# A second DRAM copy of the RWKV values, laid out by head of the pair, from which the recurrence loads

## The chip, the cores and the metric

One NeuronCore of a Trainium2 chip runs the whole layer. The metric is device microseconds (us) of one execution, the median over several runs. TensorE (PE) does the matrix products, VectorE (DVE), ScalarE (ACT) and GpSimd (POOL) the elementwise work, and SyncE (SP) issues most DMAs; ACT issues some of the stores. All DMAs of the core run on the same 16 DMA engines.

## The reference, cut to what matters

One layer of a hybrid decoder: dilated sliding-window attention and RWKV-7 time mixing run in parallel on the same 1024 tokens x 1024 features, are merged by sigmoid gates, and a squared-ReLU MLP follows. The change touches the values `v` of the RWKV part: 16 heads of 64 features, kept as 8 pairs of heads. Per head the recurrence is

```
r, k, v, fw, fa, fg = split(token_shift(f_rwkv))
def step(state, inp):
    sa = einsum('bhij,bhj->bhi', state, -kk_t)
    state = (state * w_t[:, :, None, :]
             + sa[..., None] * (kk_t * a_t)[:, :, None, :]
             + v_t[..., None] * k_t[:, :, None, :])
    y_t = einsum('bhij,bhj->bhi', state, r_t)
...
bonus = sum(r * k * r_k, axis=-1, keepdims=True) * v
y = (layernorm_per_head(y) + bonus) * g
```

so `v` is read twice: in the recurrence, and later for the bonus term of the output.

## The kernel before, in words

The kernel is written in Bass with a tile framework. The order of TensorE and GpSimd is as the program writes it (`manual_schedule`); the order of VectorE, ScalarE and SyncE is chosen by a scheduler at build time. The program's order comes from `weave` (line 62), which takes steps of a main generator and puts steps of side generators between them.

Stages, with their place in the profiled execution: input norm and low-rank columns (to about 90 us); stage 1, the RWKV projections, eight iterations m = 0 to 7, one per pair of heads (about 90 to 404 us); attention with the inverses of the chunk matrices beside it (to 830 us); the recurrence, `Chain`, 16 chunks of 64 tokens, woven into gate and branch products (about 839 to 1104 us); merge, output projection and MLP (to the end).

Stage 1: `Project.project(m)` (line 376) runs three dense products per m (k, r, v) and `finish(m - 1)` (line 416) is the side generator beside it. In `finish` the 128 value features of a pair, token-minor after the projection, are turned by TensorE transposes to token-major in PSUM (`flip`), four 128-token tiles at a time (h = 0, 1). ScalarE copies them to the tile `VT` (line 436, one buffer: a second copy waits until the stores from the first have landed) and issues the store to `V_d` (line 437). `finish` goes on to the score blocks, which DVE masks into `sc` (line 463) and SyncE stores to `AK_d` and `TB_d` (lines 464, 465). Weight tiles `raw` (line 170, three buffers) are loaded by SyncE and split by ScalarE (`whi`, line 41) and VectorE (`wlo`, line 42).

`V_d` is [1024 tokens, 1024 features]; feature = m*128 + head-of-pair*64 + i. In stage 1 a row of a store is 128 floats (512 B).

The recurrence: `Chain.load(c)` (line 840) issues eight DMAs on SyncE for chunk c: per head of the pair hp the blocks `U` from `AR_d` and `AK_d` (64 partitions each, one run of 4 KB per partition) and the values `SV` (64 partitions: 64 tokens, 8 pairs, 64 floats), and then `TB` and `BKT` (128 partitions, 4 KB runs). In `SV` each partition takes eight runs of 64 floats (256 B), since the two heads of a pair alternate in `V_d`. The tiles have two buffers, so the load for chunk c + 2 waits for the products of chunk c. `chunk(c)` (line 858) begins with products of `SV` and `U` (line 874). Every second chunk `norm(J)` (line 901) reads `V_d` by whole rows (`vt`, line 908), and `post(J)` (line 929) turns the result and stores it to `O_d` from ScalarE (line 956); the tile `y2` that this store reads is written by the next `norm` (line 918) and the next `post` (line 953), which wait until the store has landed.

## Time and profile before

| What | us |
|---|---|
| median of 3 runs | 1954.45 |
| lowest and highest of the 3 | 1944.74, 1958.83 |
| the profiled execution's own time | 1958.2 |
| its span in the profile | 1956.5 |

The mean granted TensorE clock of the profiled execution is 0.972 of full speed. The span is the time from the first to the last recorded instruction; what lies around it is 1.7 us. A row of the profile names a line of the kernel, the engine, and output<-input by the program's tile names; a wait row names the engine that waited, its line, what ended the wait, the total in us, the number of times, and the longest.

### The profile page before, as it was taken

What the parts mean: (1) busy time and instruction counts of PE and PEld (TensorE: products, weight loads), DVE (VectorE), ACT (ScalarE), POOL (GpSimd) and SP (SyncE); (2) the same over time, 40 slices, a digit from 0 to 9 for tenths busy, and PEclk for the clock granted to TensorE, in tenths of its full rate; (3) what the DMA queues carried; (4) which work ended last, traced back from release to release, by engine and by line L of the source; (5) the groups of instructions that cost most, each with busy time, mean ns of one, the idle gap of its engine ahead of it and who ended that gap; (6) DMA issues with size and microseconds to landing.
All of it is one profiled execution on the core that took longest, in us unless ns stands there. A gap on an engine that the chain in (4) does not pass through costs nothing.

```text
span 1956.5 us, 30888 instructions
## 1 busy us (share of the span) xinstructions
PE 1850.8 (95%) x12183; PEld 1509.2 (77%) x12183; DVE 1230.8 (63%) x1857; ACT 793.7 (41%) x1379; POOL 307.4 (16%) x398
## 2 busy tenths in 40 slices
PE   8999999999999999978888899989999998999996
PEld 7888888887787887666666788767888887888885
DVE  6777777734324324436566654668777776776877
ACT  7533333323534525312222333336666655433342
POOL 2011111126141507013333300310000000000001
PEclk9999999999998999989998999999999999999998
DMA  6355556652242241399898454436454447453225
GB/s 181 92 138 139 148 151 153 153 136 69 52 141 55 69 103 40 82 240 235 209 221 208 141 197 136 148 112 229 141 162 143 153 153 241 144 187 136 87 98 182
DMA packets 324914, 283.83 MB, mean 145 GB/s; under 512 B 84926, under 2 KB 275488, under 8 KB 324384
## 3 DMA queue, kind: packets, MB, share of 16 engines
q1 hardware_dynamic: 261984, 247.76, 44.5%
q10 hardware_dynamic: 60672, 26.75, 5.1%
q0 software_dynamic: 2112, 7.34, 1.1%
q8 instruction: 96, 1.57, 0.3%
q14 instruction: 50, 0.41, 0.1%
HBM read 184.70 MB, written 96.57 MB: 144 GB/s over the span
## 4 chain that ended last, share of the span: by engine, by line
PE 76%; DMA 9%; DVE 5%; issue 4%; POOL 3%; ACT 2%; SPq 1%; ACTq 0%; DVEq 0%; POOLq 0%
PE fx L1400 16%; PE fx L1252 14%; PE pd L209 12%; PE pd L211 12%; PE pd L213 12%; DMA O_d<-y 3%; DMA SV<-V_d 2%; PE pm L460 2%; DMA U<-AK_d 1%; PE pm L430 1%; PE po L694 1%; POOL X L515 1%; SPq L501 1%; POOL tmp L514 1%; PE ppt L679 1%
## 5 line engine op out<-in xcount | busy, mean ns | idle before, releaser
L1400 PE MATMUL fx<-w2s,x 128*128 128x512 f32 (+1 forms) x1362 | 307.8, 388 | 5.9 <-DVE w2s L42 4.1
L209 PE MATMUL pd<-hhi,whi 128*128 128x512 f32 (+1 forms) x880 | 300.9, 419 | 0.4 <-DVE Q L590 0.4
L1400 PEld LDWEIGHTS fx<-w2s,x 128*128 128x128 f32 x1362 | 254.9, 189 | 59.0 <-DVE w2s L42 4.4
L211 PE MATMUL pd<-hlo,whi 128*128 128x512 f32 (+1 forms) x880 | 276.9, 392 | 1.0 <-DVE mv L125 1.0
L213 PE MATMUL pd<-hhi,wlo 128*128 128x512 f32 (+1 forms) x880 | 276.0, 391 | 0.0
L42 DVE TENSOR_TENSOR wlo<-raw,whi 128x512 fp32r<-128x512 f32 (+2 forms) x164 | 113.5, 726 | 169.9 <-ACT whi L41 167.4
L211 PEld LDWEIGHTS pd<-hlo,whi 128*128 128x128 f32 x880 | 167.6, 190 | 37.0 <-DVE mv L125 1.3
L213 PEld LDWEIGHTS pd<-hhi,wlo 128*128 128x128 f32 x880 | 167.8, 191 | 35.9
L1252 PE MATMUL fx<-xh,wop 128*128 128x512 f32 x600 | 187.7, 390 | 2.6 <-ACT e L1256 1.6
L209 PEld LDWEIGHTS pd<-hhi,whi 128*128 128x128 f32 x880 | 152.4, 191 | 33.3 <-issue 8.6
L41 ACT CAST whi<-raw 128x512 fp32r<-128x512 f32 (+2 forms) x164 | 92.2, 608 | 198.2 <-PE pd L211 147.4
L1252 PEld LDWEIGHTS fx<-xh,wop 128*128 128x128 f32 x600 | 112.6, 188 | 27.1 <-ACT e L1256 2.0
L41 ACT CAST x<-xr 128x1024 fp32r<-128x1024 f32 x56 | 59.0, 1054 | 153.2 <-issue 87.0
L1252 PE MATMUL fx<-xl,wop 128*128 128x512 f32 x300 | 116.8, 389 | 0.0
L42 DVE TENSOR_TENSOR x<-xr,x 128x1024 fp32r<-128x1024 f32 x56 | 68.4, 1222 | 62.4 <-ACT x L41 62.4
L1354 POOL TENSOR_TENSOR rs<-mv,nhalf 128x1 f32<-128x1 f32 x8 | 6.3, 789 | 629.1 <-ACT jk L1365 608.7
L1181 ACT ACTIVATE e<-e 128x512 f32<-128x512 f32 x128 | 80.2, 633 | 31.0 <-DVE e L1276 10.5
L1252 PE MATMUL fx<-mh,wop 128*128 128x512 f32 x240 | 78.1, 395 | 0.2 <-ACT e L1213 0.2
L666 DVE CUSTOM_DVE_ANT_0 sc<-psc,bias 128x128 f32<-128x128 f32 (+1 forms) x96 | 30.1, 348 | 68.5 <-PE psc L661 52.4
L471 ACT COPY BKs<-pm 128x512 f32<-128x512 f32 x32 | 18.8, 588 | 131.0 <-PE pm L469 107.6
L515 POOL TENSOR_TENSOR X<-X,tmp 128x30 f32<-128x30 f32 (+14 forms) x120 | 65.8, 548 | 9.4
L451 POOL TENSOR_TENSOR BKg<-BK,GC 128x512 f32<-128x512 f32 x32 | 38.6, 1206 | 179.8 <-PE pm L469 175.7
(301 smaller groups left out, 3522.3 us busy)
## 6 DMA issues: line engine op xcount, KB each, us to landing
raw<-in_w_in SPq DMA_DIRECT2D x60, 512.0 KB, 4.3
S_d<-e SPq DMA_DIRECT2D x112, 256.0 KB, 2.1
xr<-S_d SPq DMA_DIRECT2D x56, 512.0 KB, 3.4
raw<-in_w_ffn SPq DMA_DIRECT2D x32, 512.0 KB, 5.1
w<-in_w_ffn SPq DMA_DIRECT2D x16, 1024.0 KB, 5.7
xt<-in_x SPq DMA_DIRECT2D x16, 512.0 KB, 5.5
AR_d<-AR SPq DMA_DIRECT2D x8, 1024.0 KB, 7.3
BKT_d<-BKs ACTq DMA_DIRECT2D x32, 256.0 KB, 3.4
```

Of the source, the lines that this page charges most:

```text
L41: nc.scalar.copy(hi, raw)
L42: nc.vector.tensor_sub(lo, raw, hi)
L209: nc.tensor.matmul(o, whi[k], xh[k], start=(k == 0), stop=False)
L211: nc.tensor.matmul(o, whi[k], xl[k], start=False, stop=False)
L213: nc.tensor.matmul(o, wlo[k], xh[k], start=False, stop=(k == kt - 1))
L451: nc.gpsimd.tensor_mul(t, BK[:, csls[b], :], g.GC[:, m, csls[b]].unsqueeze(2).to_broadcast([128, 4, 128]))
L460: nc.tensor.matmul(pair[hp][:, i * 128:(i + 1) * 128], BK[side[hp], cc, :], AR[side[hp], cc, :], start=True, stop=True)
L515: nc.gpsimd.tensor_add(X[:, s + 1:32, 0:s], X[:, s + 1:32, 0:s], tv)
L666: nc.vector.tensor_tensor_reduce(out=sc[:, c0:256], in0=pair[hp][:, c0:256], in1=bias[:, h, c0:256], scale=1.0, scalar=3.0e38, op0=ALU.add ...
L1181: self.g.nc.scalar.activation(t, t, f)
L1252: nc.tensor.matmul(out, op[:, w, k, :], xop[v][:, k, :], start=(n == 0 and not add), stop=(n == 11), skip_group_check=add)
L1400: nc.tensor.matmul(po[:, cols], x[:, xi, ts], w[:, wi, cols], start=(first and m == 0), stop=(last and m == 2), skip_group_check=more)
```

## The change

The values are stored twice. A DRAM tensor `VC_d` [1024 tokens, 2 heads of the pair, 8 pairs, 64] is added. In `finish`, after the store of `VT` to `V_d`, SyncE issues two more stores of the same `VT`, one per head of the pair; each moves 128 partitions x 4 tiles x 64 floats (runs of 256 B, 128 KB in all). Over m = 0 to 7 and h = 0, 1 these are 32 DMAs, 4.2 MB. `Chain.load` takes `SV` from `VC_d`: one run of 512 floats (2 KB) per partition instead of eight runs of 256 B. `norm` goes on reading `V_d`. No computing instruction is added or removed; line numbers after the first insertion shift by 1, after the second by 3, from line 1460 on by 4.

```diff
@@ finish
         vd = g.V_d.rearrange("(j p) c -> p j c", p=128)[:, :, m * 128:(m + 1) * 128]
+        vc = g.VC_d.rearrange("(j p) h m i -> p j h m i", p=128)
...
             nc.scalar.dma_start(vd[:, 4 * h:4 * h + 4, :], VT)
+            for hp in range(2):
+                nc.sync.dma_start(vc[:, 4 * h:4 * h + 4, hp, m, :], VT[:, :, side[hp]])
@@ Chain.load
-        vd = g.V_d[c * 64:(c + 1) * 64, :].rearrange("t (m h i) -> t h m i", m=8, h=2)
+        vd = g.VC_d[c * 64:(c + 1) * 64]
@@ layer
         g.V_d = dr.tile([1024, 1024], F32, name="V_d")
+        g.VC_d = dr.tile([1024, 2, 8, 64], F32, name="VC_d")
```

The orders of TensorE and GpSimd stay as they were. The scheduler's order on the other three moves in a few places.

SyncE's queue in stage 1, where an iteration's two weight loads stand; `raw` is a weight tile, `AK_d` and `TB_d` are the score stores. Before:

```order
L465 DMA TB_d<-sc_2020 64x4x128
L464 DMA AK_d<-sc_2024 64x4x128
L465 DMA TB_d<-sc_2024 64x4x128
L170 DMA raw<-in_w_in 128x8x128 x2
L464 DMA AK_d<-sc_2256 64x4x128
```

Now:

```order
L468 DMA TB_d<-sc_2033 64x4x128
L467 DMA AK_d<-sc_2037 64x4x128
L468 DMA TB_d<-sc_2037 64x4x128
L170 DMA raw<-in_w_in 128x8x128
L440 DMA VC_d<-VT 128x4x64 x2
L170 DMA raw<-in_w_in 128x8x128
L440 DMA VC_d<-VT 128x4x64 x2
L467 DMA AK_d<-sc_2273 64x4x128
```

The pair of stores of h = 0 stands between the two weight loads, the pair of h = 1 behind the second.

SyncE's queue at the end of stage 1 (m = 7); the first `raw` loads are weights of the attention. Before:

```order
L464 DMA AK_d<-sc_3578 64x4x128
L465 DMA TB_d<-sc_3578 64x4x128
L170 DMA raw<-in_w_in 128x8x128 x2
L464 DMA AK_d<-sc_3729 64x4x128
L465 DMA TB_d<-sc_3729 64x4x128
```

Now, the last rows of the stage, with the first loads of the inverses (`Dg`) behind them:

```order
L468 DMA TB_d<-sc_3846 64x4x128
L467 DMA AK_d<-sc_3850 64x4x128
L468 DMA TB_d<-sc_3850 64x4x128
L170 DMA raw<-in_w_in 128x8x128
L504 DMA Dg<-TB_d 32x16x32 x2
```

The second weight load has moved from ahead of the last 16 score stores to behind them, and four stores to `VC_d` stand ahead of these.

VectorE in the recurrence, between chunk 8 and chunk 9 (the only place where the recurrence's own steps change places with each other, and not only with a weight split); `stG` is the decayed state, `RS` the input to the next product, `yt` the output being normed. Before:

```order
L885 COPY SV<-pr 64x512
L811 TENSOR_TENSOR gs<-gs,pd 128x1024
L42 TENSOR_TENSOR wlo<-raw,whi 128x128 x2
L893 TENSOR_TENSOR SV<-pst,stG 64x512 x2
L869 TENSOR_TENSOR stG<-SV,GC 64x512 x2
L925 TENSOR_TENSOR yt<-yt,rs 128x1024
L876 TENSOR_TENSOR RS<-pr,INV_590 128x512
L926 TENSOR_TENSOR yt<-yt,vt 128x1024
```

Now:

```order
L888 COPY SV<-pr 64x512
L814 TENSOR_TENSOR gs<-gs,pd 128x1024
L42 TENSOR_TENSOR wlo<-raw,whi 128x128 x2
L896 TENSOR_TENSOR SV<-pst,stG 64x512 x2
L928 TENSOR_TENSOR yt<-yt,rs 128x1024
L872 TENSOR_TENSOR stG<-SV,GC 64x512 x2
L929 TENSOR_TENSOR yt<-yt,vt 128x1024
L879 TENSOR_TENSOR RS<-pr,INV_591 128x512
```

The two steps on `yt` have moved ahead of `stG` and of `RS`.

## Rows read from the trace of the kernel before

**Rows 1.** The page: span of the profiled execution.

```profile
span 1956.5 us, 30888 instructions
```

**Rows 2.** Busy time by stretch: stretch, length, PE PEld DVE ACT POOL, PEclk, DMA share, GB/s.

```profile
90.00:404.00 314.00, 314.00 (x1822) 254.77 (x1822) 232.80 (x320) 110.11 (x174) 35.68 (x35) 1.00 0.56 143
839.00:901.00 62.00, 46.83 (x720) 39.76 (x718) 28.78 (x37) 12.15 (x20) 9.68 (x4) 0.86 1.08 226
901.00:1104.00 203.00, 176.91 (x2313) 136.41 (x2314) 130.67 (x156) 50.26 (x86) 66.93 (x26) 0.92 0.83 207
```

**Rows 3.** What TensorE waited for, 839 to 902 us.

```profile
PE pr L874 <- DMA SV<-V_d: 12.9, 6, 6.2
```

**Rows 4.** Chain that ended last, 838 to 903 us: start, length, what.

```profile
864.43 12.87 DMA SV<-V_d
...
889.44 11.84 DMA SV<-V_d
```

**Rows 5.** Busy time by stretch, six stretches inside 849 to 900 us (columns as above).

```profile
849.00:851.00 2.00, 0.58 (x11) 0.61 (x13) 0.00 (x0) 0.00 (x0) 0.00 (x0) 0.50 1.02 383
876.00:881.00 5.00, 4.01 (x64) 3.77 (x64) 1.56 (x3) 0.00 (x0) 0.00 (x0) 0.50 1.03 201
888.00:892.00 4.00, 2.66 (x74) 2.31 (x69) 3.90 (x4) 1.16 (x2) 2.11 (x1) 1.00 1.05 211
870.00:876.00 6.00, 0.00 (x0) 0.00 (x0) 2.88 (x4) 1.11 (x2) 0.00 (x0) 0.72 1.14 202
881.00:888.00 7.00, 7.00 (x107) 5.99 (x107) 3.45 (x6) 1.64 (x2) 3.15 (x2) 0.87 1.13 193
893.00:900.00 7.00, 5.46 (x84) 4.25 (x81) 3.89 (x6) 2.74 (x4) 0.00 (x0) 1.00 1.12 199
```

**Rows 6.** DMA packets in 881 to 888 us, and in 876 to 881 us.

```profile
DMA packets 1358, 1.35 MB, mean 193 GB/s; under 512 B 1096, under 2 KB 1096, under 8 KB 1357
...
DMA packets 299, 1.00 MB, mean 201 GB/s; under 512 B 54, under 2 KB 54, under 8 KB 299
```

**Rows 7.** What TensorE and ScalarE waited for, 902 to 1104 us.

```profile
PE pst L889 <- ACT SV L884: 11.0, 4, 4.6
PE po L948 <- ACT y L953: 5.1, 1, 5.1
...
ACT y L918 <- DMA O_d<-y: 36.4, 4, 11.7
```

**Rows 8.** Stage 1, one iteration: ScalarE and TensorE by time; DMA busy tenths, 133 to 141 us.

```profile
134.31 0.37 ACTq L437 DMA_DIRECT2D V_d<-VT  x1
...
139.09 0.57 ACT L436 COPY VT<-pm 128x512 f32<-128x512 f32 x1
...
142.88 1.16 PE L460 MATMUL pm<-AR,BK 64*128 64x128 f32 x16
...
DMA  0000000000079997000000000000000000004594
```

**Rows 9.** DMA issues of the whole span: tile, queue, count, KB each, median us to landing.

```profile
AR_d<-AR SPq DMA_DIRECT2D x8, 1024.0 KB, 7.3
...
AK_d<-sc SPq DMA_DIRECT2D x64, 128.0 KB, 2.9
...
SV<-V_d SPq DMA_DIRECT2D x32, 128.0 KB, 8.2
```

**Rows 10.** End of stage 1: SyncE's two weight loads, and ScalarE's split of the second.

```profile
391.40 14.69 SPq L170 DMA_DIRECT2D raw<-in_w_in  x2
...
450.49 1.14 ACT L41 CAST whi<-raw 128x512 fp32r<-128x512 f32 x2 [8.83 <-PE pd L211]
```

**Rows 11.** Recurrence, 985 to 994 us: GpSimd, VectorE and TensorE by time.

```profile
985.83 2.35 POOL L924 TENSOR_TENSOR yt<-yt,lnw 128x1024 f32<-128x1024 f32 x1
...
986.61 2.84 DVE L869 TENSOR_TENSOR stG<-SV,GC 64x512 f32<-64x512 f32 x2
...
992.82 1.15 PE L883 MATMUL pr<-RS,TB 64*64 64x64 f32 x32
```

## The prediction

> **What bounds the kernel now.** I read the stretches first, then the waits of the two that the change touches, then the chain of waits, and last the DMA rates inside the worst stretch. TensorE sets the time nearly everywhere: in stage 1, where the new stores go, it is busy 314.0 of 314.0 us while the DMA engines carry a share of 0.56 [rows 2]. The place where it is not is the beginning of the recurrence. From 839 to 901 us the DMA share is 1.08, so the engines never rest, and TensorE is busy 46.8 of 62.0 us; of the 15.2 us left, 12.9 are six waits for `SV` [rows 2, 3]. The chain of waits runs there through transfers alone: three links of about 12 us each, all called `SV`, from 864.43 to 889.44 + 11.84 = 901.3 us [rows 4]. About eight DMAs are in flight at a time, so a link of 12 us is not the cost of a 128 KB transfer; it is the time that the eight DMAs of a chunk take together. What bounds this stretch is therefore the rate of the DMA engines, and the question is how much of it the short runs of `SV` use up. After 901 us the DMA share is 0.83 and TensorE no longer waits for `SV`; it waits behind ScalarE, which waits for the stores of `O_d` [rows 2, 7].

> **What the loads lose by their short runs.** Inside the stretch the rate falls in steps. Where only 128-partition tiles move it is 383 GB/s; where the 64-partition `U` runs of 4 KB dominate it is 201 to 211; where the 256 B runs of `SV` are mixed in it is 193, 199 and 202 [rows 5]. That those stretches are the ones with `SV` is seen in the packet counts: 1096 packets under 512 B in 881 to 888 us, which is the 1024 of one chunk (2 DMAs x 128 KB / 256 B) and some small ones, against 54 in 876 to 881 us [rows 6, 9]. So for a chunk I ask how long the same bytes would have taken at 211 GB/s: 193 x 7 = 1351 KB take 6.40 us in place of 7.0; 199 x 7 = 1393 KB take 6.60 in place of 7.0; 202 x 6 = 1212 KB take 5.74 in place of 6.0 [rows 5]. The mean gain is (0.60 + 0.40 + 0.26) / 3 = 0.4 us per chunk. The trace has no 2 KB run to 64 partitions, so this is bounded from both sides. The best that the rows allow is that the 262 KB of `SV` move at 383 and the other 1089 KB at 211: 0.68 + 5.16 = 5.84 us, a gain of 1.2. The worst that I admit is a loss as large as the expected gain, 0.4, since no row excludes it. I take 0.4 gained, because the 4 KB runs to the same 64 partitions are the nearest row, and they go at 201 to 211.

> [...] The stretches at 201 to 211 GB/s are those of 64-partition loads and the one at 383 is that of 128-partition loads [rows 5]. [...]

> **The sum, part by part.**
> - Loads of chunks 0 to 4, the five that lie in 839 to 901 us: 5 x 0.4 = 2.0 us gained. Bounds: 2.0 lost, 6.0 gained.
> - After 901 us TensorE waits 11.0 us behind `SV` copies on ScalarE and 5.1 us behind line 953, five waits in all, and ScalarE stands because stores of `O_d` land late (36.4 us in four waits) [rows 7]. Such a wait is about as long as one chunk's loads, so at most 0.4 x 5 = 2.0 us come back; as the engines are not full here (0.83) I take 1.0. Bounds: 0 and 5 x 1.2 = 6.0.
> - The 32 new stores, 16,384 packets of 256 B, 4.2 MB: taken at nothing. They stand in stage 1, where `VT` is copied at 134 and 139 us of an iteration, and between the two the DMA engines are idle after the old store has gone out [rows 8]. SyncE's next weight load stands behind the first pair; it waits for VectorE until about 391.40 + 14.69 - 0.4 = 405.7 us in the last iteration, and the stores are issued before such a load is due [rows 10].
> - The end of stage 1: the second weight load moves behind 16 score stores, from 405.7 to about 420 us. Its split begins at 450.49 [rows 10]. 30 us of cover; nothing. Bounds for both parts on stage 1: 0 and 1.0 lost.
> - VectorE's order at 986 us: `yt` now stands ahead of `stG` and `RS`. It can begin when GpSimd is done, 985.83 + 2.35 = 988.18. If `stG` keeps its 2.84 us and the other three steps take 1.2, 1.2 and 0.7, `RS` ends at 994.1, while TensorE needs it at 992.82 [rows 11]; but the two steps of `stG` overlap GpSimd's step now and would not then. I take nothing; bounds 0 and 1.3 lost.

> Sum: 2.0 + 1.0 = 3.0 us gained. The profiled execution took 1958.2 us (span 1956.5 [rows 1] and 1.7 around it), so it would take 1955.2. It lies 3.75 above the median of the runs shown, 1954.45; taken from that, the prediction is **1951.5 us**. The term bounds give 1954.45 - 12 = 1942.5 and 1954.45 + 2.0 + 1.0 + 1.3 = 1958.8.

> **Rivals.**
> - *Nothing comes back* (chance 0.22). The dips at 193 to 202 GB/s are not the short runs but halves of the tiles colliding: 64-partition loads alone also show 201 [rows 5]. Against it: the three stretches with `SV` average 198, below the others. Time 1954.5.
> - *The stall of the recurrence dissolves* (0.07). [...]
> - *The new stores hold `VT`* (0.05), the slower side. The copy of h = 1 at 139.09 us now waits for three stores and not one. Its result also frees a PSUM buffer that TensorE takes again with the score products at 142.88 [rows 8]. The copy takes 0.57, so it may begin at 142.3 at the latest; the second new store is issued at about 134.31 + 1.0 = 135.3. It decides from a landing time of 7.0 us on, and each further us costs TensorE one us in each of eight iterations. 128 KB score stores land in 2.9 us, 1 MB stores in 7.3 [rows 9]. At 9.5 us it would cost 8 x 2.5 = 20: 1974. Against it: the idle engines [rows 8].
> - *The change doesn't do what it says*: the loads still come in 256 B pieces, since the tile's row is cut by pairs. The new layout keeps the eight pairs of a head side by side, so that token and head give one run of 2 KB, and I leave it at 0.02; 1954.5.

> The forecast itself has 0.64.

> **How the numbers follow.** 1% is 19.5 us, and about what a measurement of this kernel can tell from no change. The forecast, the first and the last rival lie inside it wholly. Faster by over 1% needs more than the second rival's 16 us: I give it 0.06. Slower by over 1% is the far half of the third rival, 0.04. The rest, 0.90, is within 1%. The three runs of before spread from 1944.74 to 1958.83, that is 9.7 below and 4.4 above their median, and the range has to hold a measured median: 1942 at the low end, where the term bounds end too, and 1962 at the high one, the upper term bound and some spread. The second and third rival stay outside.

> **What would show each step right or wrong.** In the profile of the changed kernel: TensorE's waits for `SV` before 902 us fall from 12.9 to about 10 to 11; the links of the chain called `SV` fall from 12 to about 11.6; the packets under 512 B of a stretch with one chunk's `SV` fall from 1096 to under 100, and its rate rises to 205 to 211; TensorE in stage 1 stays at 314.0 of 314.0; the stores to `VC_d` land in 3 to 4 us; the first product of chunk 5 comes about 2 us earlier relative to the first of chunk 0. It is wrong if stage 1 becomes longer than 315 us, if the rate with `SV` in it stays below 203, or if the waits for `SV` vanish.

## The result, and the profile after

| Kernel | median us | lowest to highest | runs |
|---|---|---|---|
| before | 1961.50 | 1944.74 to 1971.78 | 13 |
| after | 1939.16 | 1931.97 to 1949.20 | 13 |

The ratio is 0.9915, 95% interval [0.9893, 0.9937]. A second set of eight runs of the changed kernel gave 0.9895 [0.9860, 0.9931]. So it is 0.6% to 1.1% faster by the first interval: 0.0085 x 1961.5 = 16.7 us, where the prediction had 3.0; the second set gives 0.0105 x 1957.7 = 20.6.

The same stretches as in [rows 2], after (stage 1 first, then the early and the late part of the recurrence; the columns are the same):

```profile
90.00:404.00 314.00, 314.00 (x1821) 254.77 (x1822) 232.82 (x320) 109.74 (x173) 36.01 (x35) 1.00 0.63 156
839.00:901.00 62.00, 49.98 (x796) 42.28 (x795) 32.60 (x42) 12.94 (x21) 10.04 (x4) 0.94 1.02 241
901.00:1104.00 203.00, 187.34 (x2344) 144.83 (x2344) 142.96 (x168) 56.82 (x94) 70.50 (x28) 0.97 0.79 216
```

Stage 1 has not moved: TensorE is busy 314.0 of 314.0 us with 32 more DMAs beside it. All of the gain lies in the recurrence: its last chunk begins at 1070.5 us instead of 1089.6, and the span is 1937.5 us instead of 1956.5. In the last row TensorE is busy 187.3 of 203.0 us where it was 176.9, and its granted clock is 0.97 where it was 0.92. That row is a fixed stretch of time and holds more of the later work than before; the experiments compare the same chunks instead.

What TensorE waited for at the start of the recurrence, 838 to 902 us (answers to [rows 3]), and the waits of both engines from 901 to 1104 us (answers to [rows 7]), after:

```profile
PE pr L877 <- DMA SV<-VC_d: 7.2, 3, 5.4
...
ACT y L921 <- DMA O_d<-y: 32.4, 5, 8.1
...
PE pst L892 <- ACT SV L887: 4.8, 3, 2.2
```

The waits for `SV` are 7.2 us, not 12.9; those for the copies of ScalarE 4.8, not 11.0; the wait of 5.1 us at `po` is gone. These are rows of one execution. In a second profile of the same kernel (experiment 12) `SV` has only 1.2 us, and a load of `U` has the rest:

```profile
PE pr L877 <- DMA U<-AR_d: 7.4, 2, 6.8
```

So all loads together are the fairer measure, before 902 us: 13.8 us in the kernel before and 13.7 in experiment 1, which loads the same short runs, against 7.2 and 9.2 in the two profiles of the changed kernel. The waits for the copies of ScalarE are 5.6 in the second profile, near the first, but the wait at `po` is back with 6.0. In the kernel before, ScalarE waited for `O_d` on a second line too, so that the row of [rows 7] is not the whole; that other row, from 901 to 1104 us:

```profile
ACT y L953 <- DMA O_d<-y: 10.4, 1, 10.4
```

Together that is 36.4 + 10.4 = 46.8 us before and 32.4 after, but 30.0 + 12.0 = 42.0 in the second profile after. The second term is in each case a wait for the first store to `O_d`, which lands late in some executions and not in others (experiment 12).

The transfers of the early chunks, after: the chain of waits (start, length, what; answers to [rows 4]), one stretch with a chunk's `SV` by busy time ([rows 5]), the packets of that stretch ([rows 6]), and the new stores among the DMA issues:

```profile
844.52 9.40 DMA BKT<-BKT_d
853.93 9.10 DMA BKT<-BKT_d
863.73 10.79 DMA SV<-VC_d
```

```profile
870.00:875.00 5.00, 0.24 (x2) 0.27 (x2) 2.37 (x3) 0.58 (x1) 0.00 (x0) 0.70 1.05 256
...
881.00:885.00 4.00, 4.00 (x70) 3.28 (x70) 2.45 (x5) 0.03 (x1) 2.31 (x1) 1.00 1.05 255
```

```profile
DMA packets 440, 1.28 MB, mean 256 GB/s; under 512 B 64, under 2 KB 64, under 8 KB 440
```

```profile
VC_d<-VT SPq DMA_DIRECT2D x32, 128.0 KB, 3.1
```

The 1024 small packets of a chunk are gone, and in two stretches where `SV` moves the rate is now 255 and 256 GB/s, where it was 193 to 202. These two profiles lie far apart. The sizes of the packets show where `SV` moves; three such stretches between 867 and 900 us in each of the four profiles with 256 B runs and `U` in halves go at 190 to 244 GB/s, mean 213, and in each of the four with 2 KB runs at 225 to 262, mean 241 (these profiles are listed under the experiments). The two stretches between them have means of 211 and 218. The links of the chain are 9 to 11 us long, where they were 12 to 13, and behind 875 us the chain no longer runs through transfers.

### The profile page after: what moved, and what is told of

Its sections match the earlier page's. It is cut to its first block, busy times and chain, and to the rows that moved or that the text cites. A ratio compares the mean times of both kernels' runs of the same rounds, so it can differ in the third digit from the quotient of the medians.

```text
span 1937.5 us, 30964 instructions
## 1 busy us (share of the span) xinstructions
PE 1845.8 (95%) x12183; PEld 1503.0 (78%) x12183; DVE 1234.9 (64%) x1857; ACT 793.7 (41%) x1379; POOL 306.7 (16%) x398
## 4 chain that ended last, share of the span: by engine, by line
PE 79%; DMA 6%; DVE 5%; issue 4%; POOL 3%; ACT 2%; SPq 1%; ACTq 0%; DVEq 0%; POOLq 0%
PE fx L1403 16%; PE fx L1255 14%; PE pd L209 13%; PE pd L211 12%; PE pd L213 12%; PE pm L463 2%; DMA O_d<-y 2%; DMA BKT<-BKT_d 1%; PE po L697 1%; PE pm L431 1%; POOL X L518 1%; PE ppt L682 1%; POOL tmp L517 1%; SPq L504 1%; PE po L940 1%
## 5 line engine op out<-in xcount | busy, mean ns | idle before, releaser
L454 POOL TENSOR_TENSOR BKg<-BK,GC 128x512 f32<-128x512 f32 x32 | 38.7, 1209 | 179.9 <-PE pm L472 175.8
```

The lines of the kernel that those rows point to most:

```text
L454: nc.gpsimd.tensor_mul(t, BK[:, csls[b], :], g.GC[:, m, csls[b]].unsqueeze(2).to_broadcast([128, 4, 128]))
```

## The experiments

**Where the time is, by chunks.** Each chunk of the recurrence begins with the product `pr<-SV,U`. Its rows in the timeline (start, length) at chunk 6 and at chunk 15 cut the recurrence into a part with the first store to `O_d` and a part with the five others. Before:

```profile
942.47 1.34 PE L874 MATMUL pr<-SV,U 128*64 128x64 f32 x20
...
1089.58 1.15 PE L874 MATMUL pr<-SV,U 128*64 128x64 f32 x32
```

After:

```profile
931.19 0.98 PE L877 MATMUL pr<-SV,U 128*64 128x64 f32 x26
...
1070.53 1.15 PE L877 MATMUL pr<-SV,U 128*64 128x64 f32 x32
```

So chunks 6 to 15 start to start took 147.1 us before and 139.3 after. Read in the same way from every profile, in us, with the first store to `O_d` (issued at 902 to 922 us) from issue to landing, and TensorE's waits behind ScalarE (`pst` for the `SV` copy plus `po` for `y`) in 901 to 1104 us:

| Kernel (profiles) | chunk 0 to 6 | chunk 6 to 15 | first O_d store | PE behind ACT |
|---|---|---|---|---|
| before | 95.6 | 147.1 | 16.6 | 16.1 |
| stores only (256 B runs) | 91.3 | 149.9 | 17.1 | 19.3 |
| 512 B runs | 92.6 | 143.6 | 15.5 | 11.8 |
| 1 KB runs | 89.8 | 140.1 | 17.4 | 14.7 |
| after, 2 KB (two) | 81.1, 88.8 | 139.3, 138.8 | 6.8, 17.9 | 4.8, 11.6 |
| sums in place, 256 B (two) | 88.4, 80.1 | 128.4, 126.8 | 6.8, 17.6 | 0, 0 |
| sums in place, 2 KB (two) | 81.3, 84.1 | 127.5, 128.0 | 17.2, 5.9 | 0, 0 |
| U over 128 partitions, 256 B | 74.1 | 136.4 | 6.0 | 4.4 |
| U over 128 partitions, 2 KB | 69.7 | 133.8 | 5.9 | 2.6 |
| both, 2 KB (two) | 72.0, 74.0 | 126.7, 126.7 | 6.0, 6.3 | 0, 0 |

The right part tells kernels apart to about 2 us; the left part varies by some 8 us between two profiles of one kernel. The first store falls into the left part and is 9.8 us longer in the first profile before than in the first after, so the 95.6 and 81.1 of these two are no fair pair; the last column holds the `po` wait that goes with a late first store.

Chunks 6 to 15 hold the same 1729 or 1730 recorded products in every kernel. Their stretch before, after, and with the sums in place and 256 B (second profile); columns as in [rows 2]:

```profile
942.47:1089.58 147.11, 130.70 (x1729) 101.73 (x1728) 92.78 (x112) 35.50 (x60) 47.34 (x18) 0.92 0.83 204
...
931.19:1070.53 139.34, 127.67 (x1730) 98.74 (x1729) 99.00 (x117) 35.41 (x60) 46.07 (x19) 0.96 0.81 220
...
929.31:1056.11 126.80, 122.09 (x1729) 94.54 (x1728) 94.09 (x115) 35.99 (x60) 51.07 (x20) 1.00 0.98 246
```

TensorE is idle in 16.4, 11.7 and 4.7 us of it, and the same products take 130.7, 127.7 and 122.1 us at a granted clock of 0.92, 0.96 and 1.00. The runs behind the table follow.

**1. The stores alone.** The new stores stay, and the loads go to the old layout again:

```diff
-        vd = g.VC_d[c * 64:(c + 1) * 64]
+        vd = g.V_d[c * 64:(c + 1) * 64, :].rearrange("t (m h i) -> t h m i", m=8, h=2)
```

> The 32 new stores stay, the recurrence loads SV from V_d in 256 B runs as before. Theory (the loads' short runs carry the whole difference): as before, ratio 0.998 to 1.003; the recurrence from the first product of chunk 0 to that of chunk 15 takes about 243 us as before and not 220; TensorE in stage 1 stays at 314.0 of 314.0. Rival (the stores' place moves the build order, and that order is what gains): ratio about 0.9915, as the changed kernel.

Measured 1954.04 us, ratio 0.9996 [0.9969, 1.0022]. From the first product of chunk 0 to that of chunk 15 it took 241.2 us, near the 242.7 before. The stores cost nothing that can be measured, nor does what they move in the order of stage 1. The order in the recurrence is not tested here: in the trace of this run VectorE's swap between chunks 8 and 9, and the places of two loads of `U` in SyncE's queue behind it, are those of the kernel before, while in the changed kernel they are the new ones. So the rival that this order gains stays open for experiments 2 and 3.

**2, 3. Runs of 512 B and of 1 KB.** `VC_d` is cut into q = 4 or 2 pieces, so that a row of `SV` is four runs of 512 B or two of 1 KB; the stores carry the same runs as in the changed kernel:

```diff
-        g.VC_d = dr.tile([1024, 2, 8, 64], F32, name="VC_d")
+        g.VC_d = dr.tile([1024, q, 2, 8 // q, 64], F32, name="VC_d")
```

> VC_d laid out so that SV comes in runs of 512 B (four per partition), all else and the order of all engines as in the changed kernel. Theory (each packet has a fixed cost beside its bytes, so the loss is linear in packets: 1024, 512, 256, 128 per chunk): (1024 - 512) / (1024 - 128) = 0.57 of the gain, ratio about 0.995. Rival (a threshold: only runs under 512 B are slow): the whole gain, 0.9915. Rival (the order gains, not the runs): 0.9915 as well, but then stores_only has it too.

> The same with runs of 1 KB (two per partition). Theory of linear cost: (1024 - 256) / (1024 - 128) = 0.86 of the gain, ratio about 0.993. Threshold at 512 B: 0.9915, same as run512.

Measured 1947.03 us, 0.9954 [0.9925, 0.9982], and 1943.54 us, 0.9934 [0.9905, 0.9963]. With 2 KB runs it was 0.9915. 512 B brings about half of the gain and each doubling a little more, as the theory of linear cost had it (0.995 and 0.993): no step at one size. Neighbouring sizes lie within each other's intervals; the column of chunks 6 to 15 goes the same way: 149.9 and 147.1, 143.6, 140.1, 139. Here VectorE and SyncE have the order of the changed kernel, so from 512 B to 2 KB it is the run length alone that takes off 4.5 us (one profile at 512 B). What the new order brings is contained in the step from 148.5 to 143.6, and no run separates it from the runs. Against a large share of it: 5.4 of the 9.5 us gained in chunks 6 to 15 come behind the first product of chunk 10, after VectorE's swap.

**4. The wait of ScalarE on `O_d` taken away, with the short runs.** In `post`, ScalarE copies the gated and transposed outputs of 128 tokens into `oT`, which is stored to `O_d`. `oT` has one buffer, and it is that of `y2`, the squares of the next block's norm (line 918). So ScalarE, at these squares, waits until the store has landed (36.4 us in four waits), and what stands behind them in its queue waits too, the copy of `SV` that TensorE needs among it (11.0 us of TensorE's waits) [rows 7]. Here the transposed outputs go back into the rows `yf` that they came from, a tile with three buffers, so that neither the squares nor the next `post` write what the store reads (the expectations call this "the sums in place", which is not what the edit does). VectorE's order between chunks 8 and 9 moves with this edit too, in the same way in both kernels of experiments 4 to 7. The loads have 256 B runs:

```diff
-            oT = one.tile([128, 8, 128], F32, name="y2")
+            oT = yf.rearrange("p (k t) -> p k t", k=8)
```

> The kernel before, but the turned result of post is put back into its own yt tile and stored to O_d from there, so that neither the next norm nor the next post waits for that store (y2 is no longer shared). Theory (most of what came back after 901 us are waits of ScalarE for O_d stores, passed on to TensorE): ScalarE's 36.4 us of waits at line 918 vanish, TensorE's waits behind SV L884 and L948 fall from 16 to about 4, 8 to 12 us gained, ratio 0.994 to 0.996. Rival (the waits for O_d only cover other waits of the same length, for loads or for the recurrence's own chain): under 3 us, ratio above 0.9985.

Measured 1929.31 us, 0.9851 [0.9824, 0.9878]: more than the change itself brought, and about three times what I had expected. What TensorE and ScalarE wait for in the second profile of this kernel, 901 to 1104 us, has no line of an `O_d` store left, and none of TensorE behind ScalarE; the busy time is:

```profile
901.00:1104.00 203.00, 190.16 (x2406) 148.46 (x2406) 145.35 (x178) 61.73 (x100) 71.41 (x28) 0.99 0.90 236
```

The granted clock is 0.99 here, with the old short runs, and 0.99 and 1.00 in chunks 6 to 15 of the two profiles; so the lower clock of [rows 2], 0.92, went with the waits.

**5 to 7. The same edit with 2 KB runs, twice, beside its twin.**

> The changed kernel, with the sums of the normalization put in place of their own operand, so that ScalarE no longer waits for the store to O_d. Theory (the shorter loads of the values gain mostly because the recurrence waits for loads and for the stores that queue behind them): without the wait on O_d the recurrence is bound by TensorE's own work, so that the two gains overlap: between 0.980 and 0.985 of the kernel before (the same edit on the kernel before alone gave 0.985), and the 16 chunks take 213 to 217 us. Rival (the gains are of different places and add up): 0.985 x 0.9915 = 0.977, and the 16 chunks take about 205 us.

Measured 1929.37 us, 0.9863 [0.9838, 0.9888]. This fits neither: the 2 KB runs added nothing to experiment 4. As the intervals were from two sets of runs, both kernels were run once more side by side.

> The kernel before with the sums in place, timed once more beside its twin with the short loads changed. Theory (the 2 KB runs gain only through loads and stores that ScalarE waits for, and that wait is gone here): the same time as the twin within 0.002, both 0.985 to 0.986. Rival (the two profiled executions, 1931.2 and 1923.0 us, are right, and the loads gain 8 us of their own): this one 0.985 to 0.987, the twin 0.981 to 0.983.

> The changed kernel with the sums in place, beside its twin. Theory: 0.985 to 0.986, no faster than the twin. Rival: 0.981 to 0.983.

Measured 1928.90 us, 0.9852 [0.9828, 0.9877], with 256 B runs and 1928.80 us, 0.9856 [0.9830, 0.9881], with 2 KB runs. The theory held. Both kernels of the pair have the same order of VectorE and SyncE in the recurrence, so this pair differs in the run length and the new stores alone. The two profiled executions of the first try had differed by 8 us (1931.2 and 1923.0); those of the second try differ by 5 the other way round (1922.2 and 1927.6). Without ScalarE's wait on `O_d`, the run length of the loads is worth nothing that these runs can tell (each interval is 0.0025 wide to either side, 5 us); with it, the whole change was worth 16.7.

**8, 9. U over 128 partitions.** The r and k blocks of a pair of heads are stored beside each other, so that one DMA of 128 partitions fetches what two of 64 did, six DMAs per chunk and not eight; with 2 KB and with 256 B runs of the values:

```diff
-            nc.sync.dma_start(U[side[hp], hp], g.AR_d[side[hp], c])
-            nc.sync.dma_start(U[side[1 - hp], hp], g.AK_d[side[1 - hp], c])
+            nc.sync.dma_start(U[:, hp], g.U_d[hp][:, c])
```

> The changed kernel, with the r and k rows of each pair of heads laid beside each other in DRAM, so that the loads of U fill 128 partitions in 6 transfers per chunk in place of 8. Theory (in the stage where loads bound the chunks, bytes at the rate of 128-partition loads, some 380 GB/s against 255 at best for 64 partitions): 0.5 MB of U per chunk take 1.4 us where they took 2.1 to 2.6, about 1 us of each of the five to six early chunks: 5 to 6 us, 0.988 to 0.989 of the kernel before. Rival (halves of 64 partitions run beside each other already, and bytes alone count): same as the changed kernel, 0.9915 within 0.002.

Measured 1919.86 us, 0.9828 [0.9798, 0.9859]: another 17 us off the changed kernel (13 by its second ratio, 0.9895), about three times the theory. DMA packets in 850 to 900 us, in this kernel:

```profile
DMA packets 6821, 14.84 MB, mean 297 GB/s; under 512 B 606, under 2 KB 3259, under 8 KB 6815
```

In the changed kernel, and then in the kernel before, in the same stretch:

```profile
DMA packets 5049, 12.46 MB, mean 249 GB/s; under 512 B 646, under 2 KB 1926, under 8 KB 5044
```

```profile
DMA packets 8247, 11.15 MB, mean 223 GB/s; under 512 B 4674, under 2 KB 5954, under 8 KB 8242
```

These are again single profiles. Over the four profiles each with U in halves the rate of this stretch is 223 to 232 with 256 B runs and 234 to 249 with 2 KB; over the three with 2 KB and U over 128 partitions it is 297 to 304. So the longer runs bring some 12 GB/s and this edit some 60. An untested rival: in the kernel before, about eight DMAs were in flight in this stretch (an estimate: 35 issued in 50 us, 11.6 us each from issue to landing by the medians), and six larger ones per chunk may keep more bytes in flight than eight. In this kernel it was about four (33 issued, 6.1 us), as means over the stretch. No run changed the number of DMAs without the number of partitions.

> The kernel before (values loaded in runs of 256 B) with U loaded over 128 partitions. Theory (each chunk's loads are one budget: U over 128 partitions takes off more than the short runs of the values cost, and what is left hides under TensorE): 0.985 of the kernel before or below, within 0.003 of 0.983, which U over 128 partitions gave with 2 KB runs. Rival (the two gains add): 0.9828 / 0.9915 = 0.991.

Measured 1926.55 us, 0.9846 [0.9822, 0.9869]. The theory held: with U loaded fast, going from 256 B to 2 KB brings 0.9846 - 0.9828 = 0.0018, inside the intervals. The first store to `O_d` is short in all four profiles with this edit.

**10, 11. Both edits, the fastest kernel.**

> Both edits together: the sums in place, and U loaded over 128 partitions. Theory (two walls in two places: loads in the first chunks, the O_d wait later): below either alone, 0.975 to 0.980 of the kernel before. Rival (TensorE's own 189 us of work in the recurrence is the floor that the sums in place already reach): as the sums in place with the changed kernel, within 0.002.

> The fastest kernel so far once more, with more runs: 0.9775 within 0.002. It is there as the floor for the other three of this job: what they miss of it is what their loads and the O_d wait still cost.

Measured 1912.22 us, 0.9775 [0.9749, 0.9801], and 1917.50 us, 0.9780 [0.9749, 0.9810]. This is what the theory had, about 43 us below the kernel before and 27 below the changed one (0.9775 to 0.9915). So with ScalarE's wait on `O_d` gone the loads of the early chunks still cost: U over 128 partitions takes 0.9863 to 0.9775 and 0.9856 to 0.9780, and chunks 0 to 6 from 81.3 and 84.1 us to 72.0 and 74.0, where the longer runs brought nothing that could be told.

**12. The changed kernel once more.**

> The changed kernel, unaltered, profiled a second time. Theory (with 2 KB runs the recurrence from chunk 5 on waits less behind the O_d stores, in every execution): from the first product of chunk 5 to that of chunk 15 150 to 157 us (153.4 in the first profile, 168.0 and 175.8 in the two profiles with 256 B runs), 0.9915 within 0.003. Rival (the first profile caught a good execution): 162 to 170 us.

Measured 1939.61 us, 0.9895 [0.9860, 0.9931]. The time held; the profile fell into the rival's range, 166.2 us from chunk 5 to chunk 15. Chunk 5 contains the first store to `O_d`, and that one landed after 17.9 us here, after 6.8 in the first profile. Rows from the DMA issues of 901 to 925 us, of the first profile and of this one:

```profile
O_d<-y ACTq DMA_DIRECT2D x1, 512.0 KB, 6.8
```

```profile
O_d<-y ACTq DMA_DIRECT2D x1, 512.0 KB, 17.9
```

So that store belongs to the execution, not to the run length; the table cuts at chunk 6 for this reason, and there the two profiles agree (139.3 and 138.8).

## Why the prediction was right, and where its sizes were wrong

The direction was right, the gain lies in the two places named, and the new stores and the weight load cost nothing, as said. The sum was five times too small, and the time measured, 1939.2 us, lies below the range; the kernel before measured 7 us higher in this set of runs than in the three shown, so by the ratio alone the upper end of the interval, 0.9937, still touches the lower end of the range (1942 / 1954.45 = 0.9936). That it touches, by 0.0001, is luck.

- *Loads of chunks 0 to 4, taken as 0.4 us each.* Mis-sized. From the first product of chunk 2 to that of chunk 4 the four profiles with 256 B runs and U in halves took 24.4, 22.9, 25.8 and 22.2 us, the four with 2 KB runs 21.8, 21.9, 20.9 and 21.5: means 23.8 and 21.5, about 1.1 us per chunk. From chunk 0 to chunk 4 it was 53.7, 51.0, 54.4 and 48.2 against 46.5, 46.7, 48.3 and 50.0: 3.9 us by the means, with single profiles that overlap. So the size is two or three times 0.4 per chunk, and not known better. The step that failed is to ask "how long the same bytes would have taken at 211 GB/s": I took the stretches without `SV` for the ceiling of whatever moves there, and with 2 KB runs the stretches with `SV` go at 225 to 262. The ceiling was that of one execution besides: in experiment 1, with the short runs, a stretch without `SV` goes at 233. The best case of the rows, 1.2, which I had taken for a bound only, is about what came. Out of stretches with the 64-partition loads of `U` I had made a ceiling of 211 for a mix of loads to both halves of the partitions and to all 128, and that mix passes it; the measurement decides.
- *After 901 us, taken as 1.0, bounds 0 to 6.0.* This is the term that failed most. Chunks 6 to 15 went from 148.5 (mean of two profiles with 256 B) to 139.1 (mean of two with 2 KB): 9.5 us, above the upper bound. What I had written was "such a wait is about as long as one chunk's loads, so at most 0.4 x 5 = 2.0 us come back". The runs put this in its place: the exposed time here is the wait for the `O_d` stores, 20.8 us above the 127.7 that the four profiles with the sums in place show (148.5 less their mean), and the changed kernel takes 9.5 of it. Of the 9.5, 6.3 are idle time of TensorE (17.4 to 11.0 us), nearly all of it waits behind the `SV` copies (11.0 and 13.9 against 4.8 and 5.6); the other 3.1 are the same products at a higher clock (131.2 to 128.0 us of work, at 0.92 and at 0.96). I priced the waits, too low, and not what an idle TensorE loses in clock.
- *How the loads reach the stores.* With 256 B runs the five stores after chunk 5 land after a median of 7.8 and 8.8 us, with 2 KB after 7.5 and 7.0; with the sums in place after 7.9 and 9.0 against 6.6 and 6.8. ScalarE's waits for them at line 918 (921) in chunks 6 to 15 go with the run length: 36.4 and 38.7 us, 34.4, 32.2, then 32.4 and 30.0. By the means that is 6.3 us less, as much as TensorE's idle time. That the stores share the DMA engines with the chunk loads, and land earlier for that reason, is argued. Shown is that the time falls with the run length where the order is the same (512 B to 2 KB), and that with the order the same and ScalarE's wait gone nothing is left of it. How much of the 9.5 the new order brought is open.
- *The rest.* 16.7 - 9.5 = 7 us lie ahead of chunk 6, where single profiles differ by more; chunks 0 to 4 are 3.9 of it by the means above. The twins of experiments 5 to 7 differ there by 2.1 us in the mean (54.4 and 48.2 against 48.3 and 50.0), and their waits for all loads before 902 us not at all (9.9 and 9.6 against 9.0 and 10.1). Two us are within the 5 us that their times can't tell. Whether the early gain is smaller than the means of all eight say, or is lost later on, is open.
- *New stores, weight load, VectorE's order: nothing.* The first two were right: in experiment 1 the stores landed beside an unchanged time, in the changed kernel in 3.1 us, and the second weight load was issued at 419.6 (I had written about 420). VectorE's order is not tested by itself. Nothing shows a loss by it: TensorE's waits for `RS` in chunks 6 to 15 are 1.3 us in one profile of the changed kernel and none in the other.
- *The signs.* Small packets from 1096 to 64: as announced. Links of the chain: 9 to 11 us, shorter than the 11.6 announced. Waits for `SV`: 7.2 and 1.2, lower than 10 to 11; as the second profile puts them down to `U`, this sign was badly chosen. Chunk 5 two us earlier against chunk 0: no test, since stores only already showed 65.4 us for it where before had 74.8.
- *The rivals.* The second rival (chance 0.07) is the nearest in size: its 16 us give 1954.45 - 16 = 1938.5. No run shows the clock term in these 16 us; it was an estimate. In its place the same products of chunks 6 to 15 took 3.1 us less at a granted clock of 0.96 than at 0.92. Beside it the runs showed about 1.1 us per chunk in chunks 2 and 3 and 6.3 us less idle time of TensorE in chunks 6 to 15. I gave this rival little because of the 64-partition rows, 201 to 211 GB/s [rows 5], and that was the error. The other three fell.

## What to carry to other kernels

Price a faster transfer at the place where an engine waits for what shares the DMA engines with it, not only at the transfer: here ScalarE waited for a store from a reused buffer, and that wait, 20.8 us in chunks 6 to 15, was worth more than the waits for the loads, 13.8 us before 902 us. A rate seen in one profile of the slow kernel is no ceiling unless a row with the new shape shows it. An edit that moves the build order needs a run with the new order and the old transfers; the one that was meant for it here went back to the old order. When two edits take away the same wait, try them together before adding them up: 0.9915 and 0.9851 gave 0.9856 to 0.9863, and one change of buffer did more than the second copy of the data.

## What the runs showed of the hardware

- With 2 KB runs the stretches in which `SV` moves among the other loads of a chunk went at 225 to 262 GB/s (mean of twelve 241), with 256 B runs at 190 to 244 (mean 213); the stretches between them at 201 to 229 and 193 to 233. Which loads pass which, no run separates.
- The run length cost gradually from 256 B to 2 KB (0.9996, 0.9954, 0.9934, 0.9915, each within 0.003), with no step at 512 B; the first of these has the old order in the recurrence.
- Loading 512 KB of U over 128 partitions instead of twice 256 KB over 64 each raised the rate of the early chunks from 234 to 249 up to 297 to 304 GB/s and was worth about as much time as the whole change; the number of DMAs fell with it, and no run separates the two.
- The first `O_d` store of the recurrence landed after 5.9 to 6.8 or after 15.5 to 17.9 us, in two executions of the same kernel, with nothing between; one profile would have given a false cause.
- The same products of chunks 6 to 15 kept TensorE busy 131.2 us at a mean granted clock of 0.92, 128.0 at 0.96 and 122.8 at 0.99 to 1.00 (means of two, two and four profiles).
